# Down projection of a three-pass fp32 SwiGLU layer: eight quarter products per block, or seven with stored sums of the weights

## The chip, the core and the metric

The kernel runs on one core of one Trainium2 chip. The metric is device time in microseconds (us) of one execution. The five engines are PE (TensorE: matmuls; PEld is its weight load), DVE (VectorE), ACT (ScalarE), POOL (GpSimd) and SP (SyncE, which here only issues transfers). Each engine works through its own instructions in order. A transfer that has to wait for its buffer holds up what stands behind it on the same queue.

## The reference, cut to what matters

One layer of a trunk over 2176 tokens (2048 samples and 128 of a prompt), D = 1024, D_FF = 2816:

```python
mod = silu(cond) @ w_ada + b_ada          # shift1, scale1, gate1, shift2, scale2, gate2
h = rmsnorm(x, g_mix) * (1 + scale1) + shift1
p = h @ w_in                              # q, k, v (short conv, silu), z, a, b, f
o, s = bidir_delta(q, k, v, beta, log_a)  # two scans, forward and backward, chunks of 64
mix = concat(rmsnorm(o, g_o) * silu(z), fourier_mix(f))
x = x + gate1 * (mix @ w_out)
h2 = rmsnorm(x, g_ffn) * (1 + scale2) + shift2
gt, up = split(h2 @ w_gu, 2)              # 1024 -> 2 x 2816
x = x + gate2 * ((silu(gt) * up) @ w_down)   # 2816 -> 1024: the down projection
y = rmsnorm(x, g_final)
```

Everything is float32. A product is made of three passes on numbers cut in two: the high part is an ACT copy to fp32r, the low part a DVE subtraction (`split`), and hi·hi + hi·lo + lo·hi are added up in PSUM. So a 128x128 by 128x512 product is three matmuls, and each operand costs one ACT and one DVE instruction to cut.

## The kernel before, in words

The 17 tiles of 128 tokens pass these stages, told here by their time in the span: modulation, norm and the Fourier columns (0 to 190 us); the q and k projections, `qk_pass`, in eight groups of tiles n = 0 to 7 (190 to about 500), with the triangular inverses of the delta rule threaded between (`inv_...`; they are generators that `fill` advances); the v and z projections, `v_pass` (to 722); two scans; the output projection; and from about 1297 us the FFN in three blocks of 6, 6 and 5 tiles (`BLOCKS`). Here `hb` is an activation tile of the projections, loaded from `hT` on SP, and `conv_in` and `y` are the short convolution's tiles.

In each FFN block the gate and up projections run first, for 22 slices of 128 columns (`gate_up`, matmuls at L1303). They already use Strassen's seven products, with sums of weights made on DVE (`S`, `S3`) as they are needed; their weights `w_gu` come through `stage_d`, and `wh`, `wl` are pools of cut weights. The result is 22 tiles `a` of activations, 128 x (tokens of the block). Then comes the down projection in `phase_d` (matmuls at L124 through `down`). It takes two halves of 512 output columns; in a half, for each of 22 k: cut the activations of that k (`awh`, `awl`, two cuts of 128x384; in the last block one cut `a_end` of 128x640), load `w_dn` (128x512, 256 KB, on SP, a staging pool of six), cut it (`dh`, `dl`), and issue three matmuls for every tile. A weight is thus used by 18 matmuls (15 in the last block). Beside it `coming` loads and prepares the next block's inputs (`h_raw`, `h`).

After the first half each tile is multiplied by gate2 (`gy`) and stored in DRAM (`half_d`). After the second half, per tile: the stored half `y_f` and two parts `x_f` of the residual (`late_inputs`, L1442 to L1444) are added up, squares on ACT, `rstd` on POOL, and two multiplications by `gf` (L137) before the store of y. In the last block the last four k are kept back and run tile by tile, so that the tiles end one after another.

The tile framework orders every engine's instructions by program order and priority, buffers permitting. Pools give buffers out in turn: a load into the next buffer waits for the last reader of that buffer.

## Time and profile before

| what | value |
|---|---|
| median of 3 runs | 2738.77 us (2735.55 to 2742.66) |
| profiled execution | 2738.68 us |
| its span | 2736.9 us, 45396 instructions |
| granted TensorE clock, mean | 0.981 |

The span is the time from the first to the last instruction on the core; 1.8 us of the execution lie around it. A stage's rate is read from the rows by window: busy time of each engine, the granted clock (1.00 is full speed, 2.4 GHz), the busy share of the 16 DMA engines, and GB/s.

### The profile page before, as it was taken

Reading aid. Unit: us, or ns where it says so; the run is one execution under the profiler, and the core shown is the slowest. Engines: PE = TensorE matmul, PEld = TensorE weight load, DVE = VectorE, ACT = ScalarE, POOL = GpSimd, SP = SyncE. Lnnn points to the kernel's source line nnn. Section 1 sums busy time; section 2 is a strip of 40 time slices with the busy share of each in tenths; the row PEclk is TensorE's granted clock in tenths of the full one; section 3 lists DMA queues with packets and bytes.
Section 4 is the critical chain, followed back from the end, with each engine's and each line's share of the span. In section 5 each row is a group of like instructions: output and inputs, shape, how many; then the busy total and the mean of one; then the engine's idle time right before and its main releaser. Section 6 shows DMA issues by size and latency. Waiting matters only on the chain.

```text
span 2736.9 us, 45396 instructions
## 1 busy us (share of the span) xinstructions
PE 2623.5 (96%) x16041; PEld 2384.0 (87%) x16041; DVE 1790.5 (65%) x3915; ACT 1411.8 (52%) x3108; POOL 298.8 (11%) x492
## 2 busy tenths in 40 slices
PE   6999999999999999997999999999999999999998
PEld 3898998888888778875999998899999888999986
DVE  6335978627256676666777766487777557888744
ACT  7756656423488777774433344443334444444442
POOL 1211221222200022220000000020000002000001
PEclk8999999999999999998999999999999999999999
DMA  9956778765666565545222223442222354322242
GB/s 310 310 152 196 224 227 225 194 195 178 157 175 208 170 191 180 174 151 158 78 70 74 74 81 117 142 128 73 74 74 66 91 170 125 93 84 87 91 141 89
DMA packets 436112, 396.54 MB, mean 145 GB/s; under 512 B 123084, under 2 KB 359164, under 8 KB 434284
## 3 DMA queue, kind: packets, MB, share of 16 engines
q1 hardware_dynamic: 345132, 297.65, 36.7%
q0 software_dynamic: 16624, 55.85, 6.2%
q10 hardware_dynamic: 74128, 40.13, 5.1%
q8 instruction: 127, 2.08, 0.3%
q14 instruction: 101, 0.83, 0.1%
HBM read 294.74 MB, written 98.79 MB: 144 GB/s over the span
## 4 chain that ended last, share of the span: by engine, by line
PE 73%; DMA 7%; DVE 7%; ACT 6%; issue 5%; POOL 1%; SPq 0%; ACTq 0%; DVEq 0%; POOLq 0%
PE acc L124 24%; PE acc L1303 16%; PE m L1303 16%; PE m L124 15%; PE tr L127 1%; DMA z_s<-z_d 1%; ACT h L140 1%; ACT bd1r L140 1%; DMA hb<-hT 1%; ACT bd0r L140 1%; PE tr L124 1%; ACT u L140 1%; DMA y_f<-half_d 1%; DVE inv_d L130 1%; DMA w_raw<-w_in 1%
## 5 line engine op out<-in xcount | busy, mean ns | idle before, releaser
L1303 PE MATMUL m<-h,wh 128*128 128x384 f32 (+1 forms) x1848 | 455.5, 329 | 14.2 <-ACT h L140 8.2
L1303 PE MATMUL acc<-h,wh 128*128 128x384 f32 (+1 forms) x1848 | 450.1, 327 | 0.0
L140 ACT ACTIVATE wh<-S 128x512 fp32r<-128x512 f32 x264 | 163.6, 631 | 381.0 <-DVE S L130 142.9
L1303 PEld LDWEIGHTS m<-h,wh 128*128 128x128 f32 x1848 | 327.8, 189 | 19.2 <-ACT h L140 9.7
L1303 PEld LDWEIGHTS acc<-h,wh 128*128 128x128 f32 x1848 | 327.0, 189 | 1.2 <-ACT wh L140 0.7
L124 PE MATMUL acc<-hb,w_in 128*128 128x258 f32 (+1 forms) x2304 | 326.2, 298 | 1.7 <-ACT conv_in L140 1.6
L124 PEld LDWEIGHTS acc<-hb,w_in 128*128 128x128 f32 x2304 | 312.6, 195 | 10.6 <-ACT conv_in L140 2.8
L1303 PE MATMUL acc<-h,wl 128*128 128x384 f32 (+1 forms) x924 | 300.7, 327 | 5.8 <-DVE wl L130 5.8
L1303 PE MATMUL m<-h,wl 128*128 128x384 f32 (+1 forms) x924 | 302.1, 328 | 0.0
L140 ACT ACTIVATE wh<-w_gu 128x512 fp32r<-128x512 f32 x198 | 124.6, 632 | 115.2 <-issue 47.3
L130 DVE TENSOR_TENSOR wl<-S,wh 128x512 fp32r<-128x512 f32 x264 | 179.3, 687 | 7.0 <-ACT wh L140 4.8
L1303 PEld LDWEIGHTS acc<-h,wl 128*128 128x128 f32 x924 | 173.9, 189 | 6.7 <-DVE wl L130 6.7
L137 DVE SCALAR_TENSOR_TENSOR y<-conv_in,wconv,y 128x256 f32<-128x256 f32 (+1 forms) x216 | 97.7, 468 | 119.1 <-ACT conv_in L140 117.8
L1303 PEld LDWEIGHTS m<-h,wl 128*128 128x128 f32 x924 | 174.8, 189 | 0.0
L140 ACT ACTIVATE awh<-a 128x384 fp32r<-128x384 f32 x176 | 91.1, 522 | 136.6 <-PE m L124 87.1
L130 DVE TENSOR_TENSOR awl<-a,awh 128x384 fp32r<-128x384 f32 x176 | 97.0, 556 | 90.3 <-ACT awh L140 89.8
L130 DVE TENSOR_TENSOR wl<-w_gu,wh 128x512 fp32r<-128x512 f32 x198 | 135.7, 687 | 26.9 <-ACT wh L140 26.7
L130 DVE TENSOR_TENSOR S<-w_gu 128x512 f32<-128x512 f32 x132 | 91.2, 692 | 93.4 <-DMA w_gu<-w_gu 93.1
L1417 POOL DMA_DIRECT2D half_d<-gy x17 | 9.3, 548 | 1158.7 <-DVE gy L130 1158.2
L137 DVE SCALAR_TENSOR_TENSOR r<-m,nsr,pk 64x128 f32<-64x128 f32 x272 | 94.9, 349 | 48.7 <-PE m L124 44.9
L124 PE MATMUL acc<-woh,mh 128*128 128x512 f32 x272 | 112.5, 414 | 1.8 <-DVE gx L130 1.8
L137 DVE SCALAR_TENSOR_TENSOR S<-S,gl,m 128x128 f32<-128x128 f32 x272 | 82.2, 344 | 43.2 <-PE m L124 13.6
(293 smaller groups left out, 5819.7 us busy)
## 6 DMA issues: line engine op xcount, KB each, us to landing
w_gu<-w_gu SPq DMA_DIRECT2D x264, 256.0 KB
pk<-pk_d SPq DMA_DIRECT2D x68, 512.0 KB
w_dn<-w_down SPq DMA_DIRECT2D x132, 256.0 KB
hb<-hT SPq DMA_DIRECT2D x104, 258.0 KB
w_raw<-w_ada SPq DMA_DIRECT2D x32, 512.0 KB
x<-x SPq DMA_DIRECT2D x17, 512.0 KB
hT<-hi ACTq DMA_DIRECT2D x17, 512.0 KB
hT<-lo POOLq DMA_DIRECT2D x17, 512.0 KB, 5.7
```

The lines of the kernel that those rows point to most:

```text
L124: self.nc.tensor.matmul(out, lhsT=lhsT, rhs=rhs, start=start, stop=stop)
L127: self.nc.tensor.transpose(out=out, in_=in_, identity=self.c("ident")[:in_.shape[0], :in_.shape[0]])
L130: (eng or self.nc.vector).tensor_tensor(out=out, in0=a, in1=b, op=op)
L137: self.nc.vector.scalar_tensor_tensor(out=out, in0=a, scalar=s, in1=b, op0=op0, op1=op1)
L140: self.nc.scalar.activation(out=out, in_=in_, func=f, **kw)
L1303: nc.tensor.matmul(o, lhsT=w_[:, ws], rhs=h_[:, k, :sub], start=start and k == i == 0, stop=k == 3 and i == 2, skip_group_check=not start)
L1417: nc.gpsimd.dma_start(self.half_d[n], tmp)
```

## The change

The down projection of a block is made by seven products too. Its activations are cut into quarters (upper and lower half of the 22 k; first and second half of the block's tiles), its weights into b11, b12, b21, b22 (1408 x 512 each). Each product has 11 k. Three products use w_down itself (`weights`: load and cut as before); four use sums of weights: b22-b12 (n = 3), b12-b11 (n = 1), b22+b11-b12 (n = 2) and b21 minus that (n = 0). These four are made once, by `down_sums`, in 88 pieces of 128x256: each is a DVE sum, then a cut (one ACT, one DVE instruction) and a store of 256 KB of both parts to DRAM, `td`; each four pieces need two loads of 256 KB. Its steps are threaded into `qk_pass` (groups n > 3) and `v_pass`. Later every product with sums loads two ready parts (2 x 256 KB) per k and cuts only the activations. Sums of activations are made in place in the tiles `a`: one in `gate_up` (`differ`), three per k ahead of the products y and q (`second`, `first`). The order of a block is: x, z (sums 3), x again, y (sums 2), q (sums 1), p4 (sums 0), q again; the fifth tile of the last block runs beside x and q with plain weights. Pools change: staging of 5 instead of 6, `wh` 6 and `wl` 5.

```diff
+HF = FT // 2
+WBUFS = {"wh": 6, "wl": 5}
+        self.td = d([4, 2, DFF // 2, 512], F32, name="td")
+                if n > 3:
+                    next(self.sums, None)
+    def down_sums(self):
+        nc, A, pool = self.nc, self.A, self.inv
+        out = None
+        for k in range(HF):
+            for c in (0, 256):
+                if out:
+                    nc.sync.dma_start(*out)
+                raws = []
+                for r in (0, HF):
+                    raw = pool.tile([P, 2, 256], F32, tag=f"wd{r}", name="w_dn")
+                    rows = A["w_down"][(r + k) * P:(r + k + 1) * P]
+                    nc.sync.dma_start(raw, rows.rearrange("p (h c) -> p h c", h=2)[:, :, c:c + 256])
+                    raws.append(raw)
+                (b11, b12), (b21, b22) = ((x[:, 0], x[:, 1]) for x in raws)
+                yield
+                for i, (n, to, x, y, op) in enumerate(((3, b22, b22, b12, ALU.subtract), (1, b12, b12, b11, ALU.subtract),
+                                                       (2, b11, b22, b11, ALU.add), (0, b21, b21, b11, ALU.subtract))):
+                    if i:
+                        nc.sync.dma_start(*out)
+                    self.tt(to, x, y, op)
+                    hl = pool.tile([P, 2, 256], F32R, tag="wdx", name="wd_x", bufs=2)
+                    self.split(hl[:, 0], hl[:, 1], to)
+                    dst = self.td[n, :, k * P:(k + 1) * P, c:c + 256]
+                    out = dst.rearrange("x p c -> p x c"), hl.bitcast(F32)
+                    yield
+        nc.sync.dma_start(*out)
...
+                next(self.sums, None)
...
+        if differ:
+            w = differ[1]
+            at = slice(differ[0], differ[0] + w)
+            self.tt(a[:, at], a[:, :w], a[:, at], ALU.subtract)
...
-            st = self.st = self.pool(ctx, "stage_d", 6, side="left")
-            wp = self.wp = self.pool(ctx, "ffn_w", 6, side="left")
+            st = self.st = self.pool(ctx, "stage_d", 5, side="left")
+            self.wp = self.pool(ctx, "ffn_w", 6, side="left")
...
+        def sums(n, k):
+            if k % 2:
+                ws = part("wh"), part("wl")
+            else:
+                ws = [self.st.tile([P, 512], F32R, tag="st", name="d_st") for _ in range(2)]
+            for x, t in enumerate(ws):
+                nc.sync.dma_start(t.bitcast(F32), self.td[n, x, k * P:(k + 1) * P])
+            return ws
...
+        def product(banks, f, cs, ws, add=False, before=None, after=None):
+            for k in range(HF):
+                if before:
+                    before(k)
+                a = cut(acts[f + k], cs)
+                b = ws(k)
+                for n, ps in enumerate(banks):
+                    times(ps, a, n, b, not add and k == 0, k == HF - 1, add)
+                if after:
+                    after(k, a)
...
+        product(x + left, 0, slice(0, wide), partial(weights, 0, 0), after=other)
+        z = [bank() for _ in ns]
+        product(z, 0, two, partial(sums, 3))
+        product(x + left, HF, slice(0, wide), partial(weights, HF, 0), add=True)
+        product(y, 0, two, partial(sums, 2), before=second)
+        product(q, 0, one, partial(sums, 1), before=first)
+        product(p4, HF, two, partial(sums, 0), after=load_upper)
+        product(q + rest, HF, slice(0, wide), partial(weights, HF, 512), add=True, after=load_lower)
+        for n in ns:
+            last(n, lower[n], 512, v[n], v[n], q[n])
+        for ps in rest:
+            last(5, mid[0], 512, tp.tile([P, 512], F32, tag="S3", name="gy"), ps)
```

What moves on the engines is seen at three places. The first is DVE in `v_pass`, where the inverse's steps (`inv_...`) and the convolution (`y`, two per tile) alternate. Before:

```order
L130 TENSOR_TENSOR inv_m_8293<-inv_d0_7709 128x130
L130 TENSOR_TENSOR inv_m_8296<-inv_d1_7710 128x130
L130 TENSOR_TENSOR inv_d0_7709<-inv_d0_7709,inv_m_8293 128x26x5
L130 TENSOR_TENSOR inv_d1_7710<-inv_d1_7710,inv_m_8296 128x26x5
L137 SCALAR_TENSOR_TENSOR y_8178<-conv_in_8177,wconv_84,y_8178 128x256
L130 TENSOR_TENSOR inv_m_8328<-inv_d0_7709 128x108
```

And of the change, at a like place (`w_dn` are the quarters of weights, `wd_x` the two parts of a sum):

```order
L132 TENSOR_TENSOR w_dn_9233<-w_dn_9233,w_dn_9231 128x256
L132 TENSOR_TENSOR inv_d0_7978<-inv_d0_7978,inv_m_8243 128x5x26
L132 TENSOR_TENSOR inv_d1_7979<-inv_d1_7979,inv_m_8246 128x5x26
L139 SCALAR_TENSOR_TENSOR y_8084<-conv_in_8083,wconv_84,y_8084 128x256
L132 TENSOR_TENSOR w_dn_9231<-w_dn_9231 128x256
L132 TENSOR_TENSOR inv_m_8249<-inv_d0_7978 128x150
L132 TENSOR_TENSOR inv_m_8252<-inv_d1_7979 128x150
L132 TENSOR_TENSOR wd_x_9448<-w_dn_9233,wd_x_9448 128x256
```

Two rows for every sum now stand among the others, one for the sum and one for its low part. All 88 low parts lie between the second group of `qk_pass` and the end of `v_pass`: about 15 up to group 3, 22 in groups 4 to 7, 51 in `v_pass`.

The second place is the SP queue in the last block. Before, in the second half of the columns (`y_f` and `x_f` are the late inputs):

```order
L1387 DMA w_dn_28853<-w_down 128x512
L1442 DMA x_f_28782<-x1_d_103 128x512
L1387 DMA w_dn_28882<-w_down 128x512
L1443 DMA x_f_28783<-x1_d_103 128x512
L1444 DMA y_f_28784<-half_d_102 128x512
```

Of the change, at the start of product y of the last block:

```order
L1444 DMA d_st_29349<-td_103 128x512
L1444 DMA d_st_29350<-td_103 128x512
L1444 DMA d_st_29379<-td_103 128x512
L1444 DMA d_st_29380<-td_103 128x512
L1444 DMA d_st_29409<-td_103 128x512
L1444 DMA dwh_29364<-td_103 128x512
L1444 DMA dwl_29365<-td_103 128x512
L1444 DMA d_st_29410<-td_103 128x512
L1444 DMA dwh_29394<-td_103 128x512
L1444 DMA dwl_29395<-td_103 128x512
```

Two loads now stand where one was, and those into `dwh`, `dwl` (odd k) go into the same pools as the cuts of the activations.

The third place is PE in the last block. Before, the second half of one k: fifteen matmuls for a weight (`dh`, `dl`) and a cut of the activations (`a_end`), of which these are six, then the next k:

```order
L124 MATMUL acc_28577<-dl_28806,a_end_28038 128x512
L124 MATMUL m_28573<-dh_28805,a_end_28039 128x512
L124 MATMUL m_28574<-dh_28805,a_end_28039 128x512
L124 MATMUL m_28575<-dh_28805,a_end_28039 128x512
L124 MATMUL acc_28576<-dh_28805,a_end_28039 128x512
L124 MATMUL acc_28577<-dh_28805,a_end_28039 128x512
L124 MATMUL m_28573<-dh_28828,a_end_28038 128x512
```

Of the change, product y: the rest of k = 1, k = 2 and the start of k = 3 into two banks (`acc_29342`, `acc_29343`):

```order
L1456 MATMUL acc_29342<-dwl_29365,dwh_29360 128x512
L1456 MATMUL acc_29342<-dwh_29364,dwl_29361 128x512
L1456 MATMUL acc_29343<-dwl_29365,dwh_29360 128x512
L1456 MATMUL acc_29343<-dwh_29364,dwl_29361 128x512
L1456 MATMUL acc_29342<-d_st_29379,dwh_29375 128x512
L1456 MATMUL acc_29342<-d_st_29380,dwh_29375 128x512
L1456 MATMUL acc_29343<-d_st_29379,dwh_29375 128x512
L1456 MATMUL acc_29343<-d_st_29380,dwh_29375 128x512
L1456 MATMUL acc_29342<-d_st_29379,dwl_29376 128x512
L1456 MATMUL acc_29343<-d_st_29379,dwl_29376 128x512
L1456 MATMUL acc_29342<-dwh_29394,dwh_29390 128x512
L1456 MATMUL acc_29343<-dwh_29394,dwh_29390 128x512
```

A step of k is six matmuls here. The matmul right behind this piece is the first that reads `dwl_29395`; its buffer is the one that `dwl_29346` (k = 0) had, whose last reader is the third row ahead of this piece. Fourteen matmuls lie between that reader and the matmul that needs the load. In blocks 0 and 1, with three banks, it is 21, and at the start of their product y one load into staging has only five.

## Rows read from the trace of the kernel before

**Rows 1.** The page's first part: busy time, share of the span, instructions.
```profile
PE 2623.5 (96%) x16041; PEld 2384.0 (87%) x16041; DVE 1790.5 (65%) x3915; ACT 1411.8 (52%) x3108; POOL 298.8 (11%) x492
```

**Rows 2.** Windows: projections, then down stages of the three blocks, last gate/up.
```profile
core 0: us, PE busy (x) PEld busy (x) DVE busy (x) ACT busy (x) POOL busy (x), PEclk, DMA share, GB/s
190.00:722.00 532.00, 515.66 (x4134) 467.23 (x4133) 348.13 (x934) 263.22 (x550) 128.24 (x182) 0.97 0.68 193
350.00:525.00 175.00, 166.06 (x1478) 151.30 (x1478) 145.03 (x379) 101.70 (x209) 43.32 (x63) 0.96 0.79 214
525.00:722.00 197.00, 195.66 (x1261) 176.49 (x1260) 81.19 (x208) 60.20 (x136) 58.14 (x91) 0.99 0.61 171
1603.00:1783.00 180.00, 177.93 (x792) 147.51 (x791) 102.86 (x188) 81.95 (x168) 3.36 (x6) 1.00 0.39 121
2297.00:2562.00 265.00, 260.22 (x1759) 259.76 (x1759) 223.58 (x400) 117.12 (x224) 19.22 (x30) 0.99 0.33 98
2562.00:2726.00 164.00, 163.72 (x756) 137.57 (x754) 83.64 (x126) 65.40 (x111) 6.71 (x14) 1.00 0.33 108
```

**Rows 3.** Timeline of PE in the last block's down projection.
```profile
2700.17 0.84 PE L124 MATMUL m<-dh,a_end 128*128 128x512 f32 x3
...
2703.57 0.84 PE L124 MATMUL m<-dh,a_end 128*128 128x512 f32 x3
```

**Rows 4.** PE's waits in the FFN: us in total, times, longest.
```profile
PE acc L1303 <- DVE wl L130: 5.8, 3, 4.8
PE m L1303 <- ACT h L140: 3.7, 2, 3.2
PE m L1303 <- DVE h L130: 2.7, 6, 1.3
PE m L1303 <- DVE U L130: 2.2, 1, 2.2
```

**Rows 5.** Windows just after the second and the third block's start of gate/up.
```profile
1797.50:1810.00 12.50, 10.01 (x56) 9.37 (x55) 12.04 (x21) 4.76 (x12) 9.07 (x11) 1.00 0.29 98
...
2300.00:2312.50 12.50, 7.72 (x53) 7.46 (x52) 12.50 (x22) 5.60 (x14) 10.78 (x17) 0.88 0.48 145
```

**Rows 6.** Timeline: a 128x384 load issued, and its first reader (idle, releaser).
```profile
1639.44 0.33 SPq L1245 DMA_DIRECT2D h_raw<-h_d  x1
...
1641.81 0.53 ACT L140 ACTIVATE h<-h_raw 128x384 fp32r<-128x384 f32 x1 [0.92 <-DMA h_raw<-h_d]
```

**Rows 7.** Timeline: a 256 KB load issued in the last block, and its reader.
```profile
2661.82 0.37 SPq L1444 DMA_DIRECT2D y_f<-half_d  x1
...
2666.13 0.69 DVE L130 TENSOR_TENSOR x_f<-x_f,y_f 128x512 f32<-128x512 f32 x1 [0.90 <-DMA y_f<-half_d]
```

**Rows 8.** Windows: DMA rates around those two loads.
```profile
1635.00:1647.50 12.50, 12.50 (x57) 10.36 (x56) 8.78 (x17) 6.59 (x14) 0.00 (x0) 1.00 0.40 123
2657.00:2667.00 10.00, 10.00 (x46) 8.29 (x45) 5.02 (x8) 4.75 (x11) 0.00 (x0) 1.00 0.95 335
```

**Rows 9.** Windows: the fullest DMA at the start and in the projections.
```profile
10.00:20.00 10.00, 8.17 (x21) 1.77 (x21) 6.83 (x11) 6.93 (x15) 0.00 (x0) 1.00 1.05 396
550.00:575.00 25.00, 25.00 (x181) 22.77 (x180) 6.29 (x12) 9.67 (x23) 7.26 (x9) 1.00 0.94 265
```

**Rows 10.** Timeline of DVE in gate/up: instructions back to back.
```profile
1907.69 0.69 DVE L130 TENSOR_TENSOR S<-S,w_gu 128x512 f32<-128x512 f32 x1
1908.30 0.55 DVE L130 TENSOR_TENSOR U<-V,acc 128x384 f32<-128x384 f32 x1
1908.88 0.55 DVE L130 TENSOR_TENSOR U<-U,acc 128x384 f32<-128x384 f32 x1
1909.35 0.68 DVE L130 TENSOR_TENSOR wl<-S,wh 128x512 fp32r<-128x512 f32 x1
```

**Rows 11.** Groups of ACT in the projections: busy us, mean ns, idle before.
```profile
L140 ACT ACTIVATE kq<-y 128x256 f32<-128x256 f32 x64 | 26.4, 415 | 38.8 <-DVE y L137 32.8 <-DMA hb<-hT 4.0 <-DVE inv_d L130 1.0
```

**Rows 12.** The chain that ended last, in the projections: start, us, what.
```profile
401.16 12.53 DMA hb<-hT
```

**Rows 13.** Timeline of the end: PE's last matmul, DVE's last products.
```profile
2725.33 0.39 PE L124 MATMUL acc<-dh,a_end 128*128 128x512 f32 x1
...
2730.83 1.41 DVE L137 SCALAR_TENSOR_TENSOR x_f<-x_f,rstd,gf 128x512 f32<-128x512 f32 x2 [0.44 <-POOL rstd L130]
```

More of the change, by code (lines that the diff above doesn't have):

```diff
@@ L331, in phase_ab @@
             self.setp = inv.tile([P, 2, 2, 2, 2], F32, name="setp")
+            self.sums = self.down_sums()
             with ExitStack() as right:
@@ L833, in v_pass @@
                 self.fill(4.0)
+                next(self.sums, None)
             for g in groups:
@@ L892, in scan1 @@
         self.fill(1e9)
+        self.run(self.sums)
         self.inv_ctx.close()
@@ L919, in steps @@
             self.fill(8.0)
+            next(self.sums, None)
     def chunk_step(self, d, c, slot):
@@ L1287, in gate_up_raws, with gate_up @@
         return raws
-    def gate_up(self, raws, h2, a, sub, tag):
+    def gate_up(self, raws, h2, a, sub, tag, differ):
         nc = self.nc
@@ L1294, in product @@
         def product(ps, w, name, start=True):
-            wh = self.wp.tile([P, 512], F32R, tag="wh", name="wh")
-            wl = self.wp.tile([P, 512], F32R, tag="wl", name="wl")
+            wh, wl = (self.wp.tile([P, 512], F32R, tag=t, name=t, bufs=b) for t, b in WBUFS.items())
             self.split(wh, wl, w)
@@ L1307, in gate_up @@
         x, y, z, q = (self.bank(tag) for _ in range(4))
-        v, u = (p.tile([P, 512], F32, tag=n, name=n)[:, :sub] for n, p in (("V", self.tp), ("U", self.tl)))
+        v, u = (self.tp.tile([P, 512], F32, tag=n, name=n, bufs=3)[:, :sub] for n in "VU")
         a1, a2 = a[:, :sub], a[:, sub:2 * sub]
@@ L1335, in phase_d @@
         with ExitStack() as ctx:
-            tl = self.tl = self.pool(ctx, "ffn_late", 2, side="left")
-            st = self.st = self.pool(ctx, "stage_d", 6, side="left")
-            wp = self.wp = self.pool(ctx, "ffn_w", 6, side="left")
+            st = self.st = self.pool(ctx, "stage_d", 5, side="left")
+            self.wp = self.pool(ctx, "ffn_w", 6, side="left")
+            tp = self.tp = self.pool(ctx, "ffn_t", 2, side="left")
             h1 = self.pool(ctx, "ffn_h1", side="left")
-            up = self.pool(ctx, "ffn_a", side="left")
+            up = self.up = self.pool(ctx, "ffn_a", side="left")
             h2 = self.pool(ctx, "ffn_h2", side="left")
             self.hps = {n: h1 if n in ("h11", "T1") else h2 for n in SIDES}
-            tp = self.tp = self.pool(ctx, "ffn_t", 2, side="left")
             h2 = self.ffn_first(len(BLOCKS[0]) * P // 2, up)
@@ L1347, in phase_d @@
                 sub = m // 2
-                end = blk is BLOCKS[-1]
+                pairs, odd = divmod(len(blk), 2)
+                w, at = pairs * P, (pairs + odd) * P
                 acts = []
@@ L1353, in phase_d @@
                         raws = self.gate_up_raws(j)
-                    self.gate_up(raws, h2, a, sub, "acc" if j % 2 else "m")
+                    self.gate_up(raws, h2, a, sub, "acc" if j % 2 else "m", (at, w) if j < HF else None)
                     acts.append(a)
                 coming = iter(())
-                if not end:
+                if b + 1 < len(BLOCKS):
                     h2 = self.ffn_sides()
                     coming = self.ffn_next(h2, b + 1, len(BLOCKS[b + 1]) * P // 2)
-                else:
-                    def room(x):
-                        for n in SIDES[:3]:
-                            t = self.side(n, x, "a_end").rearrange("p k t -> p (k t)")
-                            yield from (t[:, i * M:i * M + m] for i in range(2))
-                    pairs = list(zip(room("h"), room("l")))
@@ L1432, in phase_d, with act_place, late_inputs @@
-                for _ in coming:
-                    pass
-    def act_place(self, up, name):
-        return up.tile([P, M], F32, tag="a", name=name, bufs=FT)[:, :512]
-    def late_inputs(self, up, t, n):
+                self.down(blk, acts, coming, b + 1 == len(BLOCKS))
+                self.run(coming)
+    def act_place(self, name):
+        return self.up.tile([P, M], F32, tag="a", name=name, bufs=FT)[:, :512]
+    def late_inputs(self, t, n):
         rows = slice(t * P, (t + 1) * P)
-        x0, x1, y0 = (self.act_place(up, name) for name in ("x_f", "x_f", "y_f"))
+        x0, x1, y = (self.act_place(name) for name in ("x_f", "x_f", "y_f"))
@@ L1442, in late_inputs @@
         self.nc.sync.dma_start(x0, self.x1_d[rows, :512])
         self.nc.sync.dma_start(x1, self.x1_d[rows, 512:])
-        self.nc.sync.dma_start(y0, self.half_d[n])
-        return x0, x1, y0
-    def down(self, ps, n, cuts, wh, wl, k):
-        for ah, al, at, w in cuts:
-            if at <= n * P < at + w:
-                ts = slice(n * P - at, (n + 1) * P - at)
-                self.mm(ps, ah[:, ts], wh, start=(k == 0), stop=False)
-                self.mm(ps, ah[:, ts], wl, start=False, stop=False)
-                self.mm(ps, al[:, ts], wh, start=False, stop=(k == FT - 1))
+        self.nc.sync.dma_start(y, self.half_d[n])
```

180 lines of the change are left out of this document (115 added, 65 removed).

## The prediction

> **What bounds the kernel now.** I read the page's first part first: PE is busy for 96% of the span, DVE for 65% and ACT for 52% [rows 1]. An average can hide stages with other limits, so the windows by stage came next. In the down stages PE is busy for 177.93 of 180 us and for 163.72 of 164 us, at a granted clock of 1.00, with the DMA engines at 0.33 to 0.39 of their time [rows 2]. There, fewer matmuls are worth their full time as long as nothing else comes last. The timeline gives their price: two like groups of matmuls start at 2700.17 and 2703.57 us with fifteen of 128x512 from the one to the other [rows 3], so 3.40 / 15 = 0.227 us each. The projections are the fuller place for transfers: DMA share 0.68 over 190 to 722 us, 0.79 in 350 to 525, with PE at 515.66 of 532 us [rows 2]. The list of waits shows what PE loses in the FFN: four groups, 14.4 us together, most of it at the turn from one block to the next [rows 4]; the windows there show PE at 10.01 and 7.72 of 12.5 us while DVE has no time free (12.04 and 12.50) [rows 5].
>
> **1. Matmuls removed.** Before: 22 k x 2 halves x 3 passes x 6 tiles = 792 for each of two blocks, 660 for the last of 5 tiles, 2244 in all. After: 7 products x 11 k x 3 passes x 3 tiles = 693 for each of two blocks; the last has two tiles in a product, 462, and the odd tile's 22 x 2 x 3 = 132. That is 1980, so 264 fewer. All have the same shape. 264 x 0.227 = **-59.9 us**. Every pass of PE that is left is work as before; the rest of the sum is what takes some of this back.
>
> **2. Loads in the last block.** Before, 256 KB fed 15 matmuls (3.40 us): 77 GB/s. Now the four products with sums load 512 KB (0.524 MB) for six matmuls (1.36 us): 385 GB/s, in 44 steps of k. They carry 23.1 MB, and the late inputs of two tiles in p4 another 1.6 MB, against 59.9 us of PE. The trace has three rates to set against that: 396 GB/s in the fullest window of its start, 335 GB/s over 10 us in the last block, 265 GB/s in the fullest stretch of the projections, at shares of 1.05, 0.95 and 0.94 [rows 8, 9]. The first two have 2 KB rows, as the stored sums have. 24.7 MB take 62.4 us by the first (+2.5) and 73.7 us by the second (+13.8). Latency says the same in another way. A load for an odd k can start when the matmul that last read its buffer is done, and is needed 14 matmuls (3.2 us) later. A load took 2.37 us from issue to its reader at 123 GB/s [rows 6, 8] and 4.31 us at 335 GB/s [rows 7, 8]. With 4.0 us and 0.2 us for the releasing matmul to end, two steps take 12/15 x 4.2 = 3.4 us in place of 2.72, which is +0.64, over 22 pairs +14. With 4.31 us and a full 0.39 us it is 3.76, +23, and the late inputs 3 more. I take **+14**, since 335 GB/s was measured in this block with loads of this shape; bounds +2 and +26.
>
> Whether a core alone goes on past that 335 is where the trace can be read two ways. The start ran 10 us at 396 GB/s [rows 9]. The Trainium skill (Perfetto Trace Analysis, section Roofline) says that 358 GB/s is a core's share when both cores of a pair use the memory, and that a single core may reach some 120% of it. The trace agrees that 358 is no ceiling, by its 396. By that ceiling, some 430 GB/s (an estimate from the Trainium skill's figure), the last block's loads would take 57 us, less than PE, and this term would be 0; by the rate measured in the block it is 14.
>
> **3. Loads in blocks 0 and 1.** Here nine matmuls (2.04 us) use 512 KB: 257 GB/s, below 335, and the lead of 21 matmuls (4.8 us) is above 4.31 us. So the steady part is hidden by PE; without this cover each microsecond that a load is late costs one, once per two k. Two places are left. At the start of y one load has five matmuls, 1.1 us, against 2.4 to 4.3 us: I take +2. In p4 three tiles' late inputs (2.4 MB) come to 5.8 MB of sums: 8.1 MB in 22.4 us of PE, 24.3 us at 335 GB/s: +2, and one more for the next block's inputs beside them. **+5 a block, +10** (bounds 2 and 20).
>
> **4. The sums in the projections.** 88 pieces. DVE: two instructions of 128x256 each. The trace has 128x512 at 0.61 us from start to start and 128x384 at 0.47 [rows 10]; on that line 128x256 comes to about 0.34 us (an estimate). 88 x 0.68 = 60 us of the 532 - 348 = 184 us that DVE is idle from 190 to 722 us. ACT: 88 x 0.415 [rows 11] = 37 of 269 us idle [rows 2]. So both engines have room. The transfers are the tight part: 44 loads and 88 stores of 256 KB each are 34.6 MB. At the fullest stretch's 265 GB/s for a share of 0.94 [rows 9], that is 282 GB/s and 123 us of a full DMA; idle are 0.32 x 532 = 170 us. By stage: 51 of 88 in `v_pass` are 20 MB, 71 us, on a share of 0.61 of 197 us, which makes 0.97. The 22 in groups 4 to 7 add 31 us to 175 us at 0.79, 0.96 [rows 2]. It fits, barely. But the loads of `hb` stand behind the new transfers on SP, which wait for DVE's sums and for their buffers; and a late `hb` is a wait that the kernel has already: one of 12.53 us lies in the chain that ended last [rows 12]. What is queued behind `hb` is the projection's matmuls, and then conv and the inverse. The bounds are 0 and two such waits, +25; I take two thirds of one, **+8**, since PE lost only 1.3 of 197 us in `v_pass` and DMA has room in the mean.
>
> **5. Sums of activations.** One more DVE instruction of at most 0.47 us in 11 slices of gate/up per block [rows 10]: 5 us where DVE has 265 - 224 = 41 us idle [rows 2]. Ahead of y one per k, ahead of q two; with a cut that is 1.4 of 2.04 us on DVE, in the last block about 1.0 of 1.36. Priced at 0; all of them uncovered would be 16 us for those in gate/up.
>
> **6. Turn of a block.** Before, six tiles were finished after the last matmul of a block; now three, the other three after p4. DVE is what PE waits for there [rows 5]. I take back somewhat less than half of the 14.4 us [rows 4]: **-6** (bounds -10 and 0).
>
> **7. The end.** Before, the tiles ended one by one; from PE's last matmul at 2725.33 us to the start of DVE's last pair it was 5.5 us [rows 13]. Now three banks end together. Eight additions or products of 0.61 us stand on DVE (4.9 us), then the chain of square, `rstd` and final products, some 2.8 us, after the matmul's own 0.4: 8.1 us. **+2** (0 to 5).
>
> **The sum**, against the profiled 2738.7 us (the median of the runs is 2738.8, so it stands for both): -59.9 + 14 + 10 + 8 - 6 + 2 = -32, **2707 us**.
>
> **The rivals.**
> - *All loads hidden.* The DMA goes on at 396 GB/s (term 2 falls to 2.5), the two blocks lose 2 each and the projections 2: 2738.7 - 59.9 + 2.5 + 4 + 2 - 6 + 2 = 2683 us. For it speaks the 396 GB/s; against it that at 335 GB/s a load already took 4.31 us, more than its lead. By the ceiling that the Trainium skill gives (Perfetto Trace Analysis, Roofline) it would come out this way. Chance 0.17.
> - *The projections pay.* The transfers of the sums bring shares of 0.96 and 0.97, where a burst must wait; `hb` comes late twice more, +25 for +8: 2724 us. For it: rows 12; against: no longer wait than that one stands in the rows, and PE is busy for 195.66 of 197 us of `v_pass`. Chance 0.16.
> - *Slower.* The products with sums run at the rate of DMA, and that rate is low. All three blocks' sums are 69.2 MB, and 6.3 MB of late inputs lie in p4: 75.5 MB against 239 us of PE. To lose all of the gain, the loads would have to cost 59.9 + 6 - 8 - 2 = 56 us, which they do at 75.5 / 295 = 256 GB/s or less; at 240 GB/s the time is 2758 us. For it: the 265 GB/s at a share of 0.94 in the projections. Against: those packets were short, and the last block ran at 335. Chance 0.07, with as much for a time within 0.3% of before (8 us, about what a measurement of this kernel can tell from no change).
>
> **How the numbers follow.** The forecast's own case, with terms 2 and 3 between their bounds, holds 0.53 and runs from 2690 to 2722. The range is to leave out 2 in 10: it reaches down past the first rival's 2683 to 2680, and up through the second rival and the worst of term 2 with term 4 (2707 + 12 + 17 = 2736) to 2738. Faster by over 0.3% are the forecast and the first two rivals, 0.86 together; 0.07 and 0.07 are left.
>
> **What would show it.** Right: the down stages of blocks 0 and 1 at about 162 us each with PE busy, the last at about 163 minus 15 plus 14; waits of PE on DMA or on cuts in y, q and p4 of the last block, at a DMA share near 0.95 there; 190 to 722 us longer by some 8 us with a share near 0.9. Wrong: no such waits in the last block and a rate above 360 GB/s (first rival); PE waiting on `hb` for 20 us more (second); DMA full at under 270 GB/s in z, y and q of blocks 0 and 1 (third). A granted clock that falls in the last block after such waits would add time that this sum has nowhere.

## The result: slower, and the profile after

The changed kernel takes 2812.34 us (median of 4 runs, 2811.87 to 2813.09) beside 2740.72 us for the kernel before in the same runs: a ratio of 1.0255, 95% interval 1.0221 to 1.0289. The forecast was 2707 us, with 2680 to 2738 as its range. The profiled execution's span is 2811.0 us, 74.1 above that of before. Of the changed kernel, the page's first part and its windows over the projections, the first two down stages, the last gate/up and the last down stage:

```profile
PE 2601.2 (93%) x15777; PEld 2346.0 (83%) x15777; DVE 1896.0 (67%) x4252; ACT 1411.0 (50%) x3193; POOL 302.0 (11%) x492
```
```profile
178.00:760.00 582.00, 536.24 (x4191) 485.99 (x4190) 408.76 (x1108) 292.73 (x640) 125.30 (x170) 0.94 0.79 236
1659.00:1846.00 187.00, 171.54 (x712) 137.20 (x711) 120.52 (x225) 75.68 (x158) 13.75 (x21) 0.95 0.73 236
2167.00:2352.00 185.00, 167.36 (x712) 132.56 (x711) 116.61 (x223) 74.38 (x157) 13.65 (x21) 0.99 0.72 234
2352.00:2629.00 277.00, 271.90 (x1833) 270.30 (x1832) 229.40 (x419) 118.98 (x227) 9.34 (x15) 0.99 0.31 92
2629.00:2797.00 168.00, 148.70 (x619) 114.47 (x617) 92.98 (x184) 63.24 (x136) 7.68 (x11) 0.98 0.74 243
```

The 264 matmuls are gone (16041 in [rows 1], 15777 now). But a down stage that had PE busy nearly throughout at a DMA share of 0.33 to 0.39 [rows 2] now has PE idle for 15 to 19 us, at a share near 0.73. PE's three largest waits in each of the three down stages, in that order (us in total, times, longest):

```profile
PE m L1456 <- DMA d_st<-td: 7.4, 3, 3.6
PE m L1456 <- DVE dwl L132: 4.1, 5, 2.0
PE acc L1456 <- DMA dwl<-td: 3.4, 2, 1.9
```
```profile
PE m L1456 <- DVE dwl L132: 5.1, 3, 2.0
PE acc L1456 <- DMA dwl<-td: 4.5, 3, 1.5
PE m L1456 <- DMA d_st<-td: 3.4, 3, 1.6
```
```profile
PE acc L1456 <- DMA dwl<-td: 9.6, 11, 2.4
PE m L1456 <- DMA dwl<-td: 3.6, 4, 1.4
PE acc L1456 <- DMA dwh<-td: 3.0, 2, 2.3
```

One such wait in the timeline of block 0, at the start of product y:

```profile
1736.43 0.32 SPq L1444 DMA_DIRECT2D d_st<-td  x1
...
1737.14 0.39 PE L1456 MATMUL m<-d_st,dwh 128*128 128x512 f32 x1
...
1741.16 0.80 PE L1456 MATMUL m<-d_st,dwh 128*128 128x512 f32 x1 [3.63 <-DMA d_st<-td]
1741.75 0.63 PE L1456 MATMUL m<-d_st,dwl 128*128 128x512 f32 x1
```

PE is out of work 1.1 us after the load was issued; the load took 4.73 us from issue to its reader. Behind the wait a matmul takes 0.63 us from start to end in place of 0.39, and the next starts 0.43 us later in place of 0.23: PE stood still, and then runs at half the clock (granted 0.50 from 1741.2 to 1743.8 us, that is 1.2 in place of 2.4 GHz), so part of the wait is paid twice. The granted clock over this whole stage is 0.95, where it was 1.00 [rows 2]: some 9 us of full clock in 187 (an estimate, 0.05 x 187).

In the last block the loads of the products y, q and p4 fill the DMA engines for 60 us:

```profile
2709.00:2769.00 60.00, 45.06 (x171) 31.71 (x171) 19.32 (x40) 13.22 (x34) 1.63 (x3) 0.96 0.96 333
```

Stage by stage, in us of the profiled executions: the projections up to the end of their last matmul, the other stages from their first matmul to the first of the next; e1 to e16 are the runs below:

| kernel | projections end | FFN starts | gate/up 0 | down 0, 1, 2 | span |
|---|---|---|---|---|---|
| before | 721.1 | 1274.0 | 330.8 | 186.5, 184.3, 153.4 | 2736.9 |
| changed | 760.4 | 1328.2 | 330.4 | 187.1, 185.2, 168.1 | 2811.0 |
| e1 sums only | 766.3 | 1320.0 | 330.6 | 186.4, 185.2, 154.1 | 2783.3 |
| e2 down only | 727.4 | 1287.2 | 329.4 | 182.8, 180.5, 165.7 | 2763.4 |
| e3 half the loads | 720.8 | 1278.4 | 329.7 | 171.0, 168.3, 150.8 | 2713.3 |
| e4 whole sums | 766.7 | 1323.2 | 330.0 | 171.7, 170.5, 144.4 | 2759.4 |
| e10 two queues | 717.9 | 1276.4 | 329.8 | 194.1, 189.7, 175.2 | 2792.3 |
| e11 six low buffers | 715.9 | 1275.5 | 329.5 | 184.2, 180.9, 163.3 | 2743.4 |
| e16 seven staging | 720.2 | 1278.8 | 330.3 | 171.6, 170.7, 159.3 | 2734.0 |
| e8 sums in gate/up | 725.1 | 1284.1 | 351.6 | 170.1, 168.3, 145.8 | 2743.2 |
| e9 one ahead | 726.9 | 1286.3 | 345.8 | 169.2, 167.4, 144.7 | 2735.2 |

Where the projections are the same program they end between 716 and 730 us, so a single profile's difference of less than some 8 us there is not read. The 74.1 us are 39.3 up to the end of the projections, 14.9 from there to the FFN, 16.2 in the down stages, 0.9 in the three gate/up stages and 2.8 at the end. The down stages were to lose 59.9 us and gained 16.2, so 76 us went into their waits.

### The profile page after: what moved, and what is told of

The parts are those of the page before. It is cut to its first block, busy times and chain, and to the rows that moved or that the text cites. A ratio compares the mean times of both kernels' runs of the same rounds, so it can differ in the third digit from the quotient of the medians.

```text
span 2811.0 us, 46317 instructions
## 1 busy us (share of the span) xinstructions
PE 2601.2 (93%) x15777; PEld 2346.0 (83%) x15777; DVE 1896.0 (67%) x4252; ACT 1411.0 (50%) x3193; POOL 302.0 (11%) x492
## 4 chain that ended last, share of the span: by engine, by line
issue 35%; PE 31%; DMA 12%; DVE 10%; ACT 6%; POOL 2%; SPq 2%; ACTq 0%; DVEq 0%; POOLq 0%
PE acc L126 10%; PE m L126 5%; PE acc L1340 5%; PE m L1340 5%; PE m L1456 3%; DMA dwl<-td 2%; DMA w_dn<-w_down 2%; PE acc L1456 2%; DVE inv_d L132 1%; DVE y L139 1%; DMA td<-wd_x 1%; PE tr L129 1%; DMA hb<-hT 1%; DVE inv_m L132 1%; ACT bd1r L142 1%
## 5 line engine op out<-in xcount | busy, mean ns | idle before, releaser
L126 PE MATMUL acc<-hb,w_in 128*128 128x258 f32 (+1 forms) x2304 | 332.4, 302 | 10.1 <-DMA hb<-hT 5.8
L126 PEld LDWEIGHTS acc<-hb,w_in 128*128 128x128 f32 x2304 | 318.3, 199 | 20.6 <-DMA hb<-hT 6.6
L142 ACT ACTIVATE dwh<-a 128x384 fp32r<-128x384 f32 (+1 forms) x231 | 114.1, 501 | 233.2 <-PE m L1456 118.7
L142 ACT ACTIVATE wh<-w_gu 128x512 fp32r<-128x512 f32 x198 | 123.7, 626 | 184.2 <-issue 152.4
L132 DVE TENSOR_TENSOR dwl<-a,dwh 128x384 fp32r<-128x384 f32 (+1 forms) x231 | 120.5, 529 | 112.9 <-PE m L1456 56.6
L1456 PE MATMUL m<-dwl,dwh 128*128 128x512 f32 x346 | 139.1, 402 | 16.4 <-DVE dwl L132 10.5
L1456 PE MATMUL m<-dwh,dwl 128*128 128x512 f32 x346 | 136.5, 395 | 0.0
```

Of the source, the lines that this page charges most:

```text
L126: self.nc.tensor.matmul(out, lhsT=lhsT, rhs=rhs, start=start, stop=stop)
L132: (eng or self.nc.vector).tensor_tensor(out=out, in0=a, in1=b, op=op)
L142: self.nc.scalar.activation(out=out, in_=in_, func=f, **kw)
L1456: nc.tensor.matmul(ps, lhsT=x[:, ts], rhs=y, start=start and i == 0, stop=stop and i == 2, skip_group_check=skip)
```

## The experiments

**The change in two parts.** e1 adds only the making of the sums to the kernel before:

```diff
+            self.sums = self.down_sums()
...
+                if n > 3:
+                    next(self.sums, None)
```

> The kernel before, with the 88 sums of the weights made in the projections and stored, and nothing that reads them. Theory (two separate prices): the projections end 39 us later and the FFN starts some 50 us later, as in the changed kernel, so about 2790 us (2775 to 2800). Rival (the 14 us that the changed kernel loses between the scans and the FFN belong to the new pools of the FFN): only the 39, 2778 us. Rival (the sums are hidden, the loss in the projections comes with the rest of the change): within 8 us of before.

Measured: 2782.81 us, ratio 1.0159 (1.0129 to 1.0189). The projections end 45 us later, and the way from there to the FFN is as long as before (553.7 us, 552.9 before): the rival on the 14 us was right in that they don't come with the sums.

e2 leaves the sums out and fills `td` from the cut weights of block 0's gate/up:

```diff
-            self.sums = self.down_sums()
+            self.sums = iter(())
...
+                for x, part in enumerate((wh, wl)):
+                    nc.gpsimd.dma_start(self.td[n, x, r * P:(r + 1) * P], part.bitcast(F32))
```

> The changed kernel without the sums in the projections; the stored array is filled in block 0's gate/up from cut weights that are there anyway, so its contents are others and the output is not the reference's. Theory (two separate prices): the FFN starts when it did before, and the three down stages take as long as in the changed kernel (187, 185 and 168 us), so about 2738.8 + 21 = 2760 us. Rival (the down stages are slow because the projections' late transfers and pools disturb them): they take 165, 162 and 143, 2695 us.

Measured: 2768.03 us, 1.0115 (1.0078 to 1.0152). Set against before less the matmuls removed (164, 162 and 138 us), the down stages lose 19, 19 and 27 us, in the changed kernel 23, 23 and 30. The medians rise by 42 us in e1 and 28 in e2, 72 in the changed kernel, so the two parts are two prices.

**What the sums cost in the projections.** e5 keeps the transfers alone, e6 the work on DVE and ACT alone, e7 puts the transfers on GpSimd's queue; each is e1 with one edit (shown cut):

```diff
 e5, in the loop over the four sums
-                    self.tt(to, x, y, op)
-                    self.split(hl[:, 0], hl[:, 1], to)
...
-                    out = dst.rearrange("x p c -> p x c"), hl.bitcast(F32)
+                    out = dst.rearrange("x p c -> p x c"), raws[n % 2]
 e6, the two loads once, and no store in the loop
+                if not raws:
...
-                    if i:
-                        nc.sync.dma_start(*out)
 e7, in down_sums
-                    nc.sync.dma_start
+                    nc.gpsimd.dma_start
```

> The kernel before, with the same 44 loads and 88 stores of 256 KB in the projections, on SP and at the same steps, but no sums: the stores take the loaded quarters as they are, and nothing reads them. Theory (SP's order: loads of hb stand behind stores that wait for DVE's and ACT's sums): the stores wait for little, the projections lose some 10 to 20 us in place of 45: 2755 us. Rival (the bytes fill the DMA engines): the 45 stay, 2783 us. Rival (DVE and ACT stand still for the sums' loads, with the convolution and the inverse behind): within 8 us of before.

> The kernel before, with the 88 sums and their cuts on DVE and ACT in the projections, but the weights loaded once and one store at the end: all of the work, none of the transfers. Theory (SP's order): within 10 us of before, 2745 us. Rival (the bytes): within 8 us of before, too. Rival (room on DVE and ACT in the projections is taken, whatever the transfers do): 25 us or more are lost, 2770 us.

> The kernel before with sums, loads and stores as in the run with the sums alone, but all 132 transfers issued on GpSimd's queue in place of SP's. Theory (SP's order): hb no longer waits behind them, the projections lose 10 to 20 us, 2755 us. Rival (the bytes, or DVE's waits for the loads): 40 us or more, 2780 us or above; more if the inverse's transfers on that queue now wait behind the stores.

Measured: e5 2772.95 us, 1.0098 (1.0061 to 1.0135); e6 2772.49 us, 1.0100 (1.0071 to 1.0128); e7 2807.14 us, 1.0220 (1.0181 to 1.0258). SP's order, my theory, is not what costs most: off SP the transfers cost more, and PE waits 7.3 us for `hb` there, 4.5 in e1. As GpSimd's queue also carries the inverse's stores, e7 does not clear SP's order altogether. By the end of the projections transfers alone cost about 30 us and work alone about 37, more together than e1's 45, and at different places. e6 has lost 31 us by the end of `qk_pass` (its last matmul on `kq` ends at 518.8 us, 487.5 before); e5 has lost nothing there (488.2) and its 30 us in `v_pass`. e6, a window and PE's timeline:

```profile
400.00:425.00 25.00, 0.00 (x0) 0.00 (x0) 22.47 (x61) 6.40 (x11) 4.70 (x11) 0.55 0.15 29
```
```profile
426.19 1.03 PE L125 MATMUL m<-inv_x,inv_bd 128*128 128x32 f32 x4 [28.03 <-DMA inv_bd<-xd]
```

PE stands for 28 us at a matmul of the inverse, with the projections' matmuls behind it, while DVE is busy for 22.5 of 25 us with sums and the inverse's steps: the inverse comes late. But e6 moves the sums as well. With no transfer to wait for, all 88 low parts lie before 410 us, where the changed kernel has 37 of them by the end of `qk_pass`; the 31 us are the price of sums that stand closer together. And e5, with the same stretches of the kernel before under it:

```profile
488.00:525.00 37.00, 23.18 (x151) 19.50 (x148) 37.00 (x120) 15.61 (x34) 5.11 (x7) 0.77 0.91 290
525.00:625.00 100.00, 97.69 (x578) 86.98 (x576) 30.09 (x57) 33.31 (x73) 28.11 (x36) 0.91 0.97 278
```
```profile
488.00:525.00 37.00, 33.26 (x199) 29.00 (x198) 34.35 (x96) 16.77 (x35) 10.18 (x16) 0.95 0.73 197
525.00:625.00 100.00, 100.00 (x640) 89.83 (x638) 31.30 (x68) 28.54 (x67) 27.46 (x34) 0.98 0.69 196
```

Here DMA is at 0.91 to 0.97 of its time, and PE loses time and clock (0.77 and 0.91, before 0.95 and 0.98). The stores come earlier too: e5's last is issued at 655 us, that of the changed kernel at 752.

Both edits leave out that the work waits for the transfers, which was the last rival of e5's expectation. The changed kernel's own trace has it: PE's two longest waits from 190 to 760 us, then DVE's for the sums' loads and for ACT's part of the cut, then pieces of the chain that ended last:

```profile
PE m L126 <- DMA inv_bd<-xd: 10.7, 1, 10.7
PE acc L126 <- DMA hb<-hT: 5.8, 1, 5.8
```
```profile
DVE w_dn L132 <- DMA w_dn<-w_down: 39.5, 12, 9.5
DVE wd_x L132 <- ACT wd_x L142: 28.9, 15, 11.4
```
```profile
348.26 7.73 DMA td<-wd_x
...
374.49 5.06 DMA td<-wd_x
...
430.10 9.80 DMA w_dn<-w_down
```

`wd_x` has two buffers, so a cut waits until an earlier store has landed, and DVE, which goes in order, stands there with the steps of the inverse behind it. The inverse's first matmul on `inv_bd` starts at 413.4 us, 381.1 before; `qk_pass` then ends 16 us late (503.8), and the other 23 us come in `v_pass`. No run changes these buffers alone, so how the 39 us divide into DVE's time, the DMA engines' time and this waiting is not shown.

**What the down stages wait for.** e3 is e2 with one part loaded for each k, used twice. e4 is the changed kernel with the sums stored whole and cut on use:

```diff
 e3
-            for x, t in enumerate(ws):
-                nc.sync.dma_start(t.bitcast(F32), self.td[n, x, k * P:(k + 1) * P])
-            return ws
+            t = part("wh") if k % 2 else self.st.tile([P, 512], F32R, tag="st", name="d_st")
+            nc.sync.dma_start(t.bitcast(F32), self.td[n, 0, k * P:(k + 1) * P])
+            return t, t
 e4, on use
+            wh, wl = part("wh"), part("wl")
+            raw = self.st.tile([P, 512], F32, tag="st", name="d_st")
+            nc.sync.dma_start(raw, self.td[n, k * P:(k + 1) * P])
+            self.split(wh, wl, raw)
+            return wh, wl
```

> As the kernel that leaves out the sums in the projections, but each product with sums loads one part (256 KB) for each k and uses it as high and low part: as many matmuls, half the bytes, half the loads; the output is not the reference's. Theory (the loads arrive late): PE's waits in the products with sums go, the stages take about 165, 163 and 141 us: 2738.8 - 60 + 10 = 2690 us. Rival (the cuts, the epilogues or the clock make the loss): the stages stay above 180, 180 and 160, 2750 us.

> The changed kernel with the sums kept whole: one 128 KB store and one DVE instruction for each of the 88, one load of 256 KB for each k in the down projection, and a cut there as for plain weights (one ACT, one DVE instruction of 128x512). Theory (transfers are the price in both places): the projections pay some 25 us in place of 53, the down stages take about 170, 168 and 148 us, so 2738.8 + 25 - 38 = 2726 us. Rival (DVE becomes the bound of products y and q, with 2.0 of 2.04 us for each k): the stages stay at 180 or more, 2755 us.

Measured: e3 2713.61 us, 0.9910 (0.9877 to 0.9943); e4 2763.30 us, 1.0089 (1.0057 to 1.0121). The down stages take 171, 168 and 151 us in e3 and 172, 171 and 144 in e4. Of the 19, 19 and 27 us that e2 loses, half the loads give back 12, 12 and 15: late loads are the larger part. The rest of e3's expectation, 6, 5 and 10 us, did not come. In e4, where no wait for a load is left, PE still waits 6.6, 5.4 and 2.4 us for DVE's low cuts. In e4 the last down stage is 9 us shorter than before, with PE busy nearly throughout and DVE not the bound:

```profile
2601.00:2745.40 144.40, 141.82 (x620) 113.77 (x618) 117.39 (x228) 86.26 (x180) 7.72 (x11) 1.00 0.64 203
```

Its projections were to cost 25 us and cost as much as those of e1 (45.6 us), with a third fewer bytes and one DVE instruction fewer for each sum; DVE waits as long there for the sums' loads (41.0 us, 42.1 in e1).

Halving the loads halves the bytes and also frees buffers, which lengthens the lead: the matmuls between the one that gives a buffer free and the one that needs the next load into it. Three edits of e2 tell these apart: the low parts on GpSimd's queue (e10), a sixth low buffer (e11), seven staging buffers and six low ones (e16).

```diff
 e10
+                eng = nc.gpsimd if x else nc.sync
+                eng.dma_start(t.bitcast(F32), self.td[n, x, k * P:(k + 1) * P])
 e11
-WBUFS = {"wh": 6, "wl": 5}
+WBUFS = {"wh": 6, "wl": 6}
-                g2 = tp.tile([P, 512], F32, tag="g2", name="g2")
+                g2 = tp.tile([P, 512], F32, tag="g2", name="g2", bufs=1)
 e16
+WBUFS = {"wh": 6, "wl": 6}
-            st = self.st = self.pool(ctx, "stage_d", 5, side="left")
+            st = self.st = self.pool(ctx, "stage_d", 7, side="left")
-                    a = up.tile([P, M], F32, tag="a", name="a", bufs=FT)
+                    a = up.tile([P, M], F32, tag="a", name="a", bufs=FT - 2) if j < FT - 2 else acts[j - 2]
```

> As the changed kernel without its sums in the projections (2768 us), but the low part of each stored sum is loaded on GpSimd's queue, the high part on SP's: the same bytes into the same buffers, two queues. Theory (the loads are late because DMA is nearly full and a buffer's lead is shorter than a load takes): no change beyond 8 us, 2765 us. Rival (the loads are late because they stand in line on SP behind loads that wait): the three down stages fall by 8 us each, 2744 us. The output is not the reference's, as in that run.

> As the changed kernel without its sums in the projections (2768 us), with a sixth buffer for the low parts (and one for gate2's rows in place of two, to make room): in the last block the load of an odd k is needed 21 matmuls after its buffer comes free, not 15. The output is not the reference's. Theory (the lead is the price): the last block's down stage falls from 166 to about 152, the others by 5 each, 2745 us. Rival (the DMA's rate is the price, share 0.95 in the last block): within 6 us of 2768.

> As the changed kernel without its sums in the projections (2768 us; down stages 183, 181 and 166 us), with seven staging buffers in place of five and six for the low parts in place of five; the room comes from two activation tiles that the last two slices share with others, so the output is not the reference's. From a buffer's release to the matmul that needs its load there are now at least 16 matmuls, not 6, and 27 where there were 22; the bytes are the same. Theory (the rate of DMA beside everything else that moves in these products): the stages stay above 178, 176 and 160 us. Rival (the lead of the buffers): 172, 170 and 152 us or less, as with half the loads.

Measured: e10 2796.65 us, 1.0207 (1.0156 to 1.0258); e11 2753.19 us, 1.0044 (1.0022 to 1.0066); e16 2737.20 us, 0.9997 (0.9978 to 1.0016). e11 left the down stages nearly as they were (the last 163 us, 166 in e2, 152 expected); the waits changed buffers. In the last block PE had waited for `dwl`; in e11 the longest waits are these:

```profile
PE acc L1463 <- DMA dwh<-td: 4.6, 3, 2.3
PE acc L1463 <- DMA d_st<-td: 3.9, 6, 1.0
PE m L1463 <- DMA d_st<-td: 3.4, 3, 1.5
```

Against the kernel before in its own runs e11 is 12 us better than e2, of which its profile has 1 us in the down stages; where the rest lies is not shown, and neither of its expectations came out.

From the stages I took the rate for the cause, and e16 refuted it for blocks 0 and 1: with the same bytes, but no load asked for less than 16 matmuls ahead, they take 172 and 171 us, about what half the loads gave. In the last block 6 of 15 us come back. There the DMA engines stay full for 70 us in e16:

```profile
2630.00:2700.00 70.00, 58.57 (x233) 42.81 (x232) 28.84 (x59) 19.98 (x49) 2.93 (x6) 0.98 0.97 337
```

So there the rate is a price as well; the other 9 us came back only with fewer bytes (e3). e3 also lengthens the leads, and what PE still waits for in e16 are loads into `dwh`, whose ring of six e16 left as it was, so how the 9 us divide is not shown.

**A version that keeps the gain?** e8 makes e4's whole sums in block 0's gate/up, in place in slots of the activations' pool, on GpSimd's queue; e9 asks for the weights one unit ahead (a unit is two loads, their four sums and the stores); e12 does that on SP's queue with three sets of buffers; e13 adds a sixth low buffer to e12; e15 is e9 with the sums on GpSimd.

```diff
 e8, cut (e9: the two loads one unit ahead, two sets)
+                for r, raw in zip((0, HF), raws):
+                    nc.gpsimd.dma_start(raw, rows.rearrange("p (h c) -> p h c", h=2)[:, :, c:c + 256])
...
+                self.tt(b22, b22, b12, ALU.subtract)
+                self.tt(b12, b12, b11, ALU.subtract)
+                self.tt(b11, b22, b11, ALU.add)
+                self.tt(b21, b21, b11, ALU.subtract)
...
+                    nc.gpsimd.dma_start(dst.rearrange("x p c -> p x c"), raw)
 e15
-            self.tt(b22, b22, b12, ALU.subtract)
+            self.tt(b22, b22, b12, ALU.subtract, eng=nc.gpsimd)
...
```

> The sums kept whole, as in the run before with whole sums, but made in block 0's gate/up (DMA share 0.25 there, PE bound), in place in two slots of the activations' pool, two transfers of 256 KB in and two out for each four sums, on GpSimd's queue. Theory (the projections' price is where the sums are made, the down stages' price is the two loads for each k): the projections as before (FFN starts near 1298 us), gate/up of block 0 up to 5 us longer, down stages 172, 170 and 144 us: 2741 - 42 + 8 = 2707 us. Rival (the sums cost as much beside gate/up, where DVE is at 73%): block 0's gate/up 20 us longer or more, 2730 us or above.

> As the run with whole sums in block 0's gate/up, but with two sets of buffers, so that the weights of a sum are asked for one unit ahead. Theory (the 21 us that this gate/up lost are DVE standing still for the sums' loads, 34.7 us in 18 waits, with the cuts of the gate/up weights behind it): most of them come back, block 0's gate/up takes 335 us or less from its first matmul, the down stages 170, 168 and 146: 2745 - 17 = 2728 us, faster than before by some 12. Rival (DVE's time for the sums itself, 30 us, or the transfers beside w_gu): 345 us or more for this stage, 2742 us.

> As the run with whole sums one unit ahead, but with their loads and stores on SP's queue, three sets of buffers, and each store issued one unit late, so that nothing on SP waits for a sum. Theory (the 15 us that block 0's gate/up still loses belong to GpSimd's queue, whose transfers make the loads of w_gu late): this gate/up takes 335 us or less, 2724 us. Rival (the bytes beside w_gu, or DVE's 30 us, whatever the queue): 343 us or more, 2734 us.

> As that run, with a sixth buffer for low parts and one for gate2's rows in place of two. Theory (the fifth buffer costs the gate/up of blocks 1 and 2 their few us: 328 and 281 against 322 and 274): those come back, and the time is 8 us below that of the run beside it. Rival (they come from the turn of the blocks and from DVE): no difference beyond 4 us.

> As the run with whole sums one unit ahead (transfers on GpSimd's queue, two sets), but the 88 sums themselves run on GpSimd, which has nothing to do in block 0's gate/up; a 128x128 sum takes it 0.49 us in the scans, so some 70 us here (an estimate). Theory (the 15 to 17 us that the sums cost there are DVE's: its time, and its standing still with the gate/up's own sums and cuts behind it): the stage takes 334 us or less, 2722 us, clear of before. Rival (the transfers beside w_gu make its loads late, whoever sums): 343 us or more, 2735 us.

Measured: e8 2745.15 us, 1.0014 (0.9994 to 1.0034); e9 2734.86 us, 0.9980 (0.9957 to 1.0002); e12 2739.04 us, 0.9991 (0.9973 to 1.0008); e13 2745.71 us, 1.0015 (0.9993 to 1.0038); e15 2745.04 us, 1.0013 (0.9997 to 1.0029). All are the kernel before, within what can be told. In e9's profile the down stages save 43 us and the projections end 6 us later, within their spread, but block 0's gate/up is 15 us longer, those of the other blocks 12 together, and the FFN starts 12 later. In e12, e13 and e15 that gate/up takes 348, 357 and 350 us: neither the queue nor DVE's waits for the sums' own loads explain it alone. In e9 the chain that ended last has the loads of `w_gu` at 18.5% of this stage, where the kernel before has matmuls at 91%; in e12, on SP's queue, it has the sums' own loads at 9.0% and their stores at 7.1%. Each edit moved the wait. e15, which was to take DVE out, slows DVE in another way (last section). e9's window in the stretch where the sums are made, and the kernel before in the same stretch:

```profile
1310.00:1500.00 190.00, 182.11 (x1011) 177.40 (x1010) 158.41 (x317) 65.27 (x121) 60.96 (x84) 0.98 0.59 182
```
```profile
1310.00:1500.00 190.00, 190.00 (x1098) 190.00 (x1097) 138.48 (x237) 75.10 (x132) 0.00 (x0) 1.00 0.26 74
```

e13 against e12 did not give its 8 us: no gain from the sixth buffer.

## Why the prediction was wrong

**Term 1 was right**: 264 fewer, and where nothing is late (e4) the last down stage falls below that of before.

**Term 4 was mis-sized: 8 us priced, 39 to 45 measured.** The step that failed is "both engines have room": 184 us of DVE idle over 532 us. The mean hid how busy DVE is where the inverse runs (145 of 175 us in 350:525 of [rows 2]), and the sum had no term for DVE standing still, 39.5 us at the sums' loads and 28.9 at their cuts, with the inverse behind it: PE waits 10.7 us for the inverse in the changed kernel, and in e6, with the sums packed closer, 28. The transfers were seen as the tight part, rightly, but a share of 0.97 worked out from means was taken as "it fits": e5 shows 30 us for them. The wait for `hb`, which I had taken for the mechanism, is 5.8 us and not the main one, and the one edit of SP's order (e7) gave nothing back. The second rival had the place right, but not its sign (20 us more of PE waiting on `hb`), and its 25 us were still too few. The division among the causes stays open.

**Term 3 failed at "the steady part is hidden": 10 us priced, 46 measured.** I compared a lead of 21 matmuls (4.8 us) with a load of 4.31 us. The lead that counts is the shortest in each pool, and it holds only if the queue is not waiting for another buffer; the timeline above has a load of 4.73 us issued 1.1 us before PE has nothing else. I had priced one such place at 2 us; it costs 3.6 us and the half clock behind it. e16 gives 11 and 10 us back in these blocks by buffers alone. Not all of the 46 are loads: in e3 some 7 us a block remain above what the matmuls need, and in the changed kernel PE waits 4.1 and 5.1 us for DVE's cuts.

**Term 2 was half its size: 14 us priced, 30 measured.** The last block's rate was worked out rightly: of the two readings, 335 GB/s held (333 over 60 us, 337 over 70 in e16), and nothing near 430 was kept up. But it was priced as another way of saying the lead; e16 gives 6 us back by buffers with the DMA engines full, so both are paid. Between e2's 166 us and the 138 that the matmuls leave, 6 go with e16's buffers and 9 more with half the loads; some 12 are left in e3, 7.0 of them waits for loads into `dwh`, the rest not taken apart.

**Term 7** was right in size (end +2.8), and so was **term 5** in gate/up (+0.9 in all), though [rows 10] have 0.58 us as well as the 0.47 for a 128x384. Its part in the down stages was put at nothing; the waits for DVE's cuts there, just named, stand mostly in the last product, while DVE finishes the tiles of p4. **Term 6** gave nothing: gate/up of blocks 1 and 2 changed by -1.1 and +2.4 us.

**What had no term**: the granted clock, named in the prediction's last sentence, some 9 us in block 0; and 14.9 us between the projections and the FFN. About 5 of these lie between the starts of the output projection's last matmul and gate/up's first (16.7 us, 11.3 before), in e2 and e4 too (16.5 and 16.4) and not in e1 (11.7), so they come with the FFN's new code and pools; the rest stays open.

In all: -59.9 + 30 + 46 + 39 + 1 + 3 + 15 = 74 us, for terms 1, 2, 3, 4, 5 with 6, and 7, and the stretch without a term.

The forecast's weakness was its rivals' prices: each was worked out with the others held at their likeliest values, but the costs of both places came together: 76 us in the down stages is more than the 56 at which the third rival said the gain is gone.

## What to carry to other kernels

Read room by stage and by chain, not by mean: an engine that is idle for a third of a pass may be busy exactly where its results are waited for, and what it is made to wait for there holds up everything behind it. When fewer matmuls share each loaded operand, price the shortest lead in every buffer ring and the time of all transfers that share the stretch, before counting the matmuls saved. And work that is made once for later has to be made somewhere: here making the sums cost 15 us at the cheapest place tried, of 43 saved; the other losses (12 us in the later gate/up stages, 12 ahead of the FFN) took the rest and were not explained.

## What the runs showed that was not expected

GpSimd's sums slow DVE's. In e15 a 128x256 sum takes GpSimd 1031 ns, and DVE's sums of SBUF operands beside it take up to twice as long; e9 and then e15, same stretch, 1350 to 1500 us:

```profile
L132 DVE TENSOR_TENSOR S<-w_gu 128x512 f32<-128x512 f32 x20 | 13.8, 692 | 25.0 <-DMA w_gu<-w_gu 24.9
L132 DVE TENSOR_TENSOR a<-a,U 128x384 f32<-128x384 f32 x10 | 5.5, 552 | 0.0
L132 DVE TENSOR_TENSOR V<-V,m 128x384 f32<-128x384 f32 x9 | 4.9, 548 | 0.0
```
```profile
L132 DVE TENSOR_TENSOR S<-w_gu 128x512 f32<-128x512 f32 x20 | 17.9, 895 | 11.7 <-DMA w_gu<-w_gu 11.6
L132 DVE TENSOR_TENSOR a<-a,U 128x384 f32<-128x384 f32 x10 | 11.1, 1111 | 0.0
L132 DVE TENSOR_TENSOR V<-V,m 128x384 f32<-128x384 f32 x10 | 5.4, 543 | 0.0
```

Sums with both operands in SBUF go from 552 to 1111 ns and from 692 to 895; the one with an operand in PSUM (`m`) stays at 543. The Trainium skill (SBUF — State Buffer, section "SBUF: two separate sides") says that DVE and GpSimd share one pair of ports, which one of them holds for a whole instruction, and that a DVE instruction needs it when it has two inputs in SBUF; the trace agrees. And loads on GpSimd's queue were no way round a busy SP: the same bytes on two queues made the down stages 9 to 11 us longer each (e10 against e2).
